# A decoder layer on one core: the GLU and the conv's gates become a stage of seven-product pairs ahead of the attention

## The chip, the cores and the metric

The kernel runs on one core of one Trainium2 chip. The metric is the time of one execution in microseconds (us), measured on the device; the median of three runs of the kernel before is 1817.19 us. The engines are named as in the profile: PE (TensorE, matmuls), PEld (its weight loads), DVE (VectorE), ACT (ScalarE), POOL (GpSimd) and SP (SyncE, which here only issues DMAs). Each engine works through its own instructions in a fixed order. ACT and POOL issue DMAs too, from the same queues as their arithmetic, so a DMA that can't be issued yet holds up what stands behind it.

## The reference

One layer of a hybrid decoder for 1024 tokens of width 1024, all in float32.

```
h = rms_norm(x)
q, k, v (12 heads of 128), glu_in (2*1024), gates (2*1024) = split(h @ w_in)
a   = dilated window attention: 3 groups of 4 heads, dilation 1, 4, 16; merged over the groups
y_a = a @ w_attn_out
c   = c_val * sigmoid(c_gate)                    # the GLU, glu_in = [c_val | c_gate]
c   = causal depthwise conv of 31 taps over c
y_c = silu(layer_norm(c)) @ conv_pw_w
mixed = sigmoid(g_a + b) * y_a + sigmoid(g_c + b) * y_c
x   = x + rms_norm(mixed @ w_out)
u   = conv of 3 taps over rms_norm(x) @ w_up     # 2 * 2816 columns
x   = x + rms_norm((gelu(u_gate) * u_val) @ w_down)
```

## The kernel before, in words

Channels lie on the 128 partitions and tokens along the free dimension, in two halves of 512. Every float32 product is made of three matmuls: each operand is split into a high part (ACT, line 166) and a low remainder (DVE, line 167), and high*high, high*low and low*high are added up in PSUM (`mm3`, lines 185 to 188). A block of 128 output channels and 512 tokens over 1024 input channels takes 24 matmuls of 128x512.

The order of the instructions on each engine is chosen at compile time by a planner, which takes the instructions in the order of the program as priorities and moves a later one forward where an engine would otherwise be free. `tc.high_priority(offset=-LAG)` puts the conv's taps 2000 places back, so that they fill what DVE has left. Inside `tc.manual_schedule()` the order is the written one.

The stages, in order:

- Norm of x (lines 211 to 235). The rows are normed and transposed into `hTh` and `hTl`. ACT issues the loads of the small tables (lines 122 to 127) in between.
- Attention (lines 244 to 451). Per group, `values_of` projects v in two halves through the two PSUM tiles `pp`, and then come four heads. `head` projects q and k (96 matmuls, through `pp`) and `core` does scores, softmax and values. The bias table goes from `sel` through DRAM (`vscr`, `bscr`), with DMAs on ACT's queue (lines 250 to 258). Between the heads stand the eight GLU blocks: `glu(m)` projects gate and value (96 matmuls), takes the sigmoid, multiplies, and hands the tile to the conv on DVE (31 taps, lines 268 to 272). `conv_out` (line 275) transposes a finished conv and stores it into `convn` in DRAM. At the end `gates(mp, 1, ..)` projects the conv's gates (384 matmuls) and stores them into `sigc`.
- Middle (lines 454 to 569). Its pool of tiles stands where the attention's stood. `weights` loads the row sums (line 470) and makes the groups' weights; `gates(mp, 0, ..)` projects the attention's gates (384 matmuls), with two `merge(n)` behind each pair of blocks. A merge loads 128 tokens of all heads (`ld`, line 492), weights and adds them on DVE, and transposes them (line 499) into `aTh` and `aTl`. Then come `y_a`, the layer norm with its transposes (`norm_half`) and the pointwise projection.
- Output projection and norms (lines 572 to 672). The last lines build sums and differences of blocks of the normed activations (T1 to T4).
- Up-projection. Two of 22 pairs of blocks go plainly (`up_plain`), the other 20 as `Seven` (line 760): a pair of 128 output channels by 1024 tokens over 1024 channels is a 2 by 2 block product, and it is made of seven block products instead of eight, each of 12 matmuls. Four sums of weight blocks are made on POOL (line 770), seven splits on ACT and DVE, and what PSUM holds is copied and added between the products (`take`). The steps have written times (`AT`, line 757): one product per step, splits five steps ahead.
- Down-projection, last norm and output.

Of the kernel before, what the change touches and what calls it, by code (L numbers as in the profile page):

```python
# [78 lines left out]
def trunk_kernel(ctx: ExitStack, tc: tile.TileContext, a, out):  # L79
# [41 lines left out]
    def small_loads():  # L121
        nc.scalar.dma_start(ffn_g, a["ffn_g"])
        nc.scalar.dma_start(conv_w, a["conv_w"])
        nc.scalar.dma_start(conv_b, a["conv_b"])
        nc.scalar.dma_start(gate_b, a["gate_b"])
        nc.scalar.dma_start(ffn_w, a["ffn_w"])
        nc.scalar.dma_start(ffn_b, a["ffn_b"])
# [71 lines left out]


    with ExitStack() as mix:
# [8 lines left out]

        with tc.tile_pool(name="xs", bufs=1) as xs:
            xt = [dt() for _ in range(NT)]
            for i in range(NT):
                nc.sync.dma_start(xt[i], a["x"][i * P:(i + 1) * P, :])
            nc.scalar.dma_start(mix_g, a["mix_g"])
            hTh += [dt(F32R) for _ in range(KC)]
            hTl += [dt(F32R) for _ in range(KC)]
            first_w = None
            for T0, n in ((0, 1), (1, 3), (4, 4)):
                rows = xt[T0:T0 + n]  # L220
                ss = xs.tile([P, 4], F32, tag="ss", name="ss", bufs=2)
                for t in range(n):
                    sq = xs.tile([P, D], F32, tag="sq", name="sq", bufs=2)
                    nc.scalar.activation(sq, rows[t], AF.Square, accum_out=ss[:, t:t + 1])
                r = rsqrt_of(ss[:, :n], 1.0 / D, RMS_EPS, xs, f"rx{n}", n)
                for t in range(n):
                    if n == 4 and t == 3:
                        nc.scalar.mul(rows[t], rows[t], r[:, t:t + 1])
                    else:
                        nc.vector.tensor_scalar(rows[t], rows[t], r[:, t:t + 1], None, op0=ALU.mult)  # L230
                ts = slice(T0 * P, (T0 + n) * P)
                transposed(rows, lambda k: (hTh[k][:, ts], hTl[k][:, ts]), mix_g)
                if not first_w:
                    first_w = [load_v(0, k) for k in range(4)]
            small_loads()

# [5 lines left out]
        bscr = dram.tile([12, P, BW[0]], F32, name="bscr")  # L242

        with tc.tile_pool(name="att", bufs=1) as att:
# [5 lines left out]
            nc.scalar.dma_start(relb[0:32, :], a["rel_bias"])  # L250
            nc.scalar.dma_start(sel, a["sel"])
# [4 lines left out]
            nc.scalar.dma_start(vscr, vrow)  # L256
            for g in range(3):
                nc.scalar.dma_start(  # L258
                    bscr[4 * g:4 * g + 4, :, :BW[g]],
                    vscr[4 * g:4 * g + 4, BOFF[g]:BOFF[g] + BW[g]].unsqueeze(1).to_broadcast((4, P, BW[g])))  # L260
# [4 lines left out]
            def conv(m, cin):  # L265
                acc = att.tile([P, S], F32, tag="acc", name="acc", bufs=2)
                with tc.high_priority(offset=-LAG):
                    nc.vector.tensor_scalar(acc, cin[:, 0:S], conv_w[:, m, 0:1], conv_b[:, m:m + 1],
                                            op0=ALU.mult, op1=ALU.add)
                    for k in range(1, TAPS):  # L270
                        nc.vector.scalar_tensor_tensor(acc, cin[:, k:k + S], conv_w[:, m, k:k + 1], acc,  # L271
                                                       op0=ALU.mult, op1=ALU.add)
                ready.append((m, cin, acc))

            def conv_out():

                m, nat, acc = ready.pop(0)
                for q in range(2):
                    pt = ps_tile((P, 4, P), "pt")
                    for k in range(4):  # L280
                        nc.tensor.transpose(pt[:, k, :], acc[:, (4 * q + k) * P:(4 * q + k + 1) * P], ident)
                    nc.scalar.copy(nat[:, q * 512:(q + 1) * 512], pt.rearrange("p a b -> p (a b)"))
                nc.gpsimd.dma_start(
                    convn.rearrange("(n p) (m c) -> p n m c", p=P, c=P)[:, :, m, :],
                    nat[:, 0:S].rearrange("p (n c) -> p n c", c=P))

            def glu(m):
                w = load_pair(a["w_glu"][m], 4)
                pv, pg = pp_tile(), pp_tile()
                cin = att.tile([P, TAPS - 1 + S], F32, tag="cin", name="cin", bufs=2)  # L290
                project(w, 1, h_in, pg)
                nc.scalar.activation(cin[:, TAPS - 1:], pg, AF.Sigmoid)
                project(w, 0, h_in, pv)
                nc.vector.memset(cin[:, 0:TAPS - 1], 0.0)
                nc.vector.tensor_mul(cin[:, TAPS - 1:], pv, cin[:, TAPS - 1:])
                conv(m, cin)
# [14 lines left out]
            def values_of(g):  # L311
# [4 lines left out]
                for half in range(2):  # L316
                    pv = [pp_tile() for _ in range(2)]
                    for k in range(KC):
                        wh, wl = first_w[k] if (g, half) == (0, 0) and k < 4 else load_v(g, k)
# [111 lines left out]
            for g in range(3):  # L431
                vt = values_of(g)
                for j in range(NH):
                    head(g, j, vt, 0 if j % 2 == 0 else len(ready) if (g, j) == (2, 3) else min(len(ready), 1))
                    for m in glus.get((g, j), ()):
                        glu(m)
# [530 lines left out]
```

## Time and profile before

| | |
|---|---|
| three runs | 1815.9, 1817.19, 1818.48 us |
| the profiled execution | 1822.72 us, of which the span of the profile 1820.6 us |
| PE busy | 1767.3 us, 97% of the span, 8152 matmuls |
| DVE busy | 1177.1 us, 65% |
| ACT busy | 720.7 us, 40% |
| POOL busy | 215.4 us, 12% |
| mean granted clock of TensorE | 0.988 |

A row of the timeline gives start, duration, engine, line, operation, tiles and count, and in brackets the time that the engine was idle before it and what ended that. A row of the windows gives the busy time of each engine in a stretch (and its instructions), then the granted clock as a share of 2.4 GHz, the busy share of the DMA engines and GB/s. A matmul's own duration overlaps the next one's: what one costs is the distance between two starts. An engine named with a q (ACTq, SPq) issues DMAs.

### The profile page before, as it was taken

Reading aid. Unit: us, or ns where it says so; the run is one execution under the profiler, and the core shown is the slowest. Engines: PE = TensorE matmul, PEld = TensorE weight load, DVE = VectorE, ACT = ScalarE, POOL = GpSimd, SP = SyncE. Lnnn points to the kernel's source line nnn. Section 1 sums busy time; section 2 is a strip of 40 time slices with the busy share of each in tenths; the row PEclk is TensorE's granted clock in tenths of the full one; section 3 lists DMA queues with packets and bytes.
Section 4 is the critical chain, followed back from the end, with each engine's and each line's share of the span. In section 5 each row is a group of like instructions: output and inputs, shape, how many; then the busy total and the mean of one; then the engine's idle time right before and its main releaser. Section 6 shows DMA issues by size and latency. Waiting matters only on the chain.

```text
span 1820.6 us, 22184 instructions
## 1 busy us (share of the span) xinstructions
PE 1767.3 (97%) x8152; PEld 1483.4 (81%) x8152; DVE 1177.1 (65%) x1967; ACT 720.7 (40%) x1331; POOL 215.4 (12%) x241
## 2 busy tenths in 40 slices
PE   7899999999989999999999999999999999999997
PEld 5688889788988888888888888778888888788886
DVE  6239979339682587947574457857667676873524
ACT  6232343243422333222442244555455555653322
POOL 0000010021100000000000000342332323120000
PEclk9999999999999999999999999999999999999998
DMA  5321133121321222235333143243323333683532
GB/s 193 111 50 51 46 85 95 35 77 48 89 76 29 68 58 82 93 109 183 116 102 118 57 146 116 83 132 99 110 87 101 98 91 128 202 286 114 179 99 93
DMA packets 84285, 188.21 MB, mean 103 GB/s; under 512 B 11331, under 2 KB 13267, under 8 KB 84176
## 3 DMA queue, kind: packets, MB, share of 16 engines
q1 hardware_dynamic: 67536, 139.75, 25.1%
q0 software_dynamic: 13392, 43.46, 7.3%
q10 hardware_dynamic: 3248, 3.58, 0.6%
q8 instruction: 64, 1.05, 0.2%
q14 instruction: 45, 0.37, 0.1%
HBM read 149.90 MB, written 38.94 MB: 104 GB/s over the span
## 4 chain that ended last, share of the span: by engine, by line
PE 61%; issue 29%; DVE 3%; POOL 3%; DMA 2%; ACT 1%; ACTq 1%; SPq 0%; POOLq 0%; DVEq 0%
PE ps L710 10%; PE pp L186 10%; PE pp L187 10%; PE pp L188 10%; PE po L710 6%; PE pt L710 4%; PE ps L188 1%; PE ps L187 1%; PE ps L186 1%; PE pp L710 1%; POOL oscr L416 1%; ACTq L258 1%; POOL mscr L416 1%; PE po L188 1%; PE pt L188 1%
## 5 line engine op out<-in xcount | busy, mean ns | idle before, releaser
L186 PE MATMUL pp<-d,wh 128*128 128x512 f32 x1088 | 430.0, 396 | 15.1 <-DVE d L332 14.8
L188 PE MATMUL pp<-d,wl 128*128 128x512 f32 x1088 | 428.9, 394 | 0.0
L187 PE MATMUL pp<-d,wh 128*128 128x512 f32 x1088 | 428.7, 394 | 0.0
L271 DVE SCALAR_TENSOR_TENSOR acc<-cin,conv_w,acc 128x1024 f32<-128x1024 f32 x240 | 305.4, 1283 | 4.6 <-issue 1.5
L186 PEld LDWEIGHTS pp<-d,wh 128*128 128x128 f32 x1088 | 206.2, 189 | 58.0 <-issue 15.7
L188 PEld LDWEIGHTS pp<-d,wl 128*128 128x128 f32 x1088 | 206.1, 189 | 41.7
L187 PEld LDWEIGHTS pp<-d,wh 128*128 128x128 f32 x1088 | 206.3, 190 | 41.2
L167 DVE TENSOR_TENSOR wl<-wr,wh 128x512 fp32r<-128x512 f32 x200 | 136.9, 689 | 153.8 <-ACT wh L166 152.7
L166 ACT CAST wh<-wr 128x512 fp32r<-128x512 f32 x200 | 123.5, 623 | 266.9 <-PE pp L187 164.0
L710 PE MATMUL ps<-d,wh 128*128 128x512 f32 x592 | 182.6, 389 | 1.3 <-ACT ps L786 1.3
L167 DVE TENSOR_TENSOR wl<-wq,wh 128x512 fp32r<-128x512 f32 x148 | 119.3, 814 | 93.5 <-ACT wh L166 93.5
L166 ACT CAST wh<-wq 128x512 fp32r<-128x512 f32 x148 | 91.5, 624 | 129.5 <-PE pt L188 100.9
L710 PEld LDWEIGHTS ps<-d,wh 128*128 128x128 f32 x592 | 111.1, 188 | 24.8 <-ACT ps L786 1.7
L167 DVE TENSOR_TENSOR wl<-ws,wh 128x512 fp32r<-128x512 f32 x80 | 63.7, 799 | 81.6 <-ACT wh L166 81.6
L710 PE MATMUL ps<-d,wl 128*128 128x512 f32 x296 | 115.3, 389 | 0.0
L687 DVE SCALAR_TENSOR_TENSOR u<-u,ffn_w 128x1023 f32<-128x1023 f32 x88 | 112.7, 1281 | 3.3 <-ACT u L681 1.9
L710 PE MATMUL po<-d,wh 128*128 128x512 f32 x336 | 103.6, 389 | 0.0
L187 PE MATMUL pp<-wl,d 128*128 128x512 f32 x232 | 91.0, 392 | 1.8 <-DVE wl L167 1.8
L188 PE MATMUL pp<-wh,d 128*128 128x512 f32 x232 | 90.7, 392 | 0.0
L186 PE MATMUL pp<-wh,d 128*128 128x512 f32 x232 | 89.6, 392 | 0.7 <-ACT u L616 0.7
L325 PE MATMUL pp<-wh,d 128*128 128x512 f32 x192 | 80.1, 418 | 3.0 <-DVE d L332 3.0
L326 PE MATMUL pp<-wl,d 128*128 128x512 f32 x192 | 79.3, 413 | 0.0
(300 smaller groups left out, 2958.4 us busy)
## 6 DMA issues: line engine op xcount, KB each, us to landing
wq<-in_w_up_dram SPq DMA_DIRECT2D x100, 256.0 KB, 2.7
wq<-in_w_down_dram SPq DMA_DIRECT2D x88, 256.0 KB, 3.2
wr<-in_w_v_dram SPq DMA_DIRECT2D x48, 256.0 KB, 2.8
wr<-in_w_qk_dram SPq DMA_DIRECT2D x48, 256.0 KB, 2.7
fscr<-u POOLq DMA_DIRECT2D x22, 512.0 KB, 2.9
d<-fscr POOLq DMA_DIRECT2D x44, 256.0 KB, 5.0
wr<-in_w_glu_dram SPq DMA_DIRECT2D x32, 256.0 KB, 2.7
wr<-in_w_gate_dram SPq DMA_DIRECT2D x32, 256.0 KB, 2.8
```

What stands on the lines that cost most here:

```text
L166: nc.scalar.copy(hi, raw)
L167: nc.vector.tensor_sub(lo, raw, f(hi))
L186: nc.tensor.matmul(ps, lh, rh, start=first, stop=False)
L187: nc.tensor.matmul(ps, lh, rl, start=False, stop=False)
L188: nc.tensor.matmul(ps, ll, rh, start=False, stop=last)
L258: nc.scalar.dma_start(bscr[4 * g:4 * g + 4, :, :BW[g]], vscr[4 * g:4 * g + 4, BOFF[g]:BOFF[g] + BW[g]].unsqueeze(1).to_broadcast((4, P, BW ...
L271: nc.vector.scalar_tensor_tensor(acc, cin[:, k:k + S], conv_w[:, m, k:k + 1], acc, op0=ALU.mult, op1=ALU.add)
L325: nc.tensor.matmul(ps, hTh[k][:, sl], wh, start=k == 0, stop=False)
L326: nc.tensor.matmul(ps, hTh[k][:, sl], wl, start=False, stop=False)
L416: nc.gpsimd.dma_start(dst[:, r, :, g, j, :], src[:, 2 * r:2 * r + 2, :])
L687: nc.vector.scalar_tensor_tensor(o[:, d:], src[:, :S - d], ffn_w[:, c, k:k + 1], o[:, d:], op0=ALU.mult, op1=ALU.add)
L710: nc.tensor.matmul(ps, wp[:, cs], xp, start=first and k == 0 and n == 0, stop=last and k == 3 and n == 2, skip_group_check=open_)
```

## The change

The eight GLU pairs and the four pairs of the conv's gates move into a stage of their own between the norm and the attention. There GLU 0 and 1 are made plainly, first for tokens 0 to 511 (whose rows are loaded and normed first), then for tokens 512 to 1023; between them the blocks of h and the sums T1 to T4 are built, into 16 tiles. Then GLU 2 to 7 and the four pairs of gates go as ten pairs of seven products, with the class `Seven` moved up and shared with the up-projection. The GLU tiles 2 to 7 are stored to DRAM (`cinscr`). The taps of convs 0 and 1 stand in this stage's written order, one tap per step. The attention keeps convs 2 to 7, loaded from `cinscr`, and no GLU. The attention's gates are projected half at the end of the attention (two pairs, before the last `conv_out`) and half in the middle, one pair ahead of merges 0 to 3 and one ahead of merges 4 to 7. The small tables and the bias table's DMAs are issued on POOL's queue.

```diff
-        nc.scalar.dma_start(ffn_g, a["ffn_g"])
+        nc.gpsimd.dma_start(ffn_g, a["ffn_g"])
...
+    def product(ps, w, X, x, first, last, open_=False):
+
+        for k in range(4):
+            cs = slice(k * P, k * P + P)
+            xh, xl = X[x, k]
+            for n, (wp, xp) in enumerate(((w[0], xh), (w[0], xl), (w[1], xh))):
+                nc.tensor.matmul(ps, wp[:, cs], xp, start=first and k == 0 and n == 0,
+                                 stop=last and k == 3 and n == 2, skip_group_check=open_)
...
+    def weave(pairs, sum_tile, extra=()):
+
+        todo = list((at, rank, -1, what) for at, rank, what in extra)
+        for n, pair in enumerate(pairs):
+            pair.n, pair.sum_tile = n, sum_tile
+            todo += [(7 * n + at, rank, n, what) for at, rank, what in pair.steps()]
+        with tc.manual_schedule():
+            for *_, what in sorted(todo, key=lambda x: x[:3]):
+                what()
...
+            for cin in cins:
+                nc.gpsimd.memset(cin[:, 0:TAPS - 1], 0.0)
+            glu_plain(0)
+            for i in range(4, 8):
+                nc.sync.dma_start(xt[i], a["x"][i * P:(i + 1) * P, :])
+            rows = norm_rows(4, 4)
...
+            wide = [u_tile() for _ in range(4)]
...
+            glu_plain(1)
...
+            class Glu(Mix):
+                def after(self):
+                    g = lambda: self.gate
+                    return ((13, lambda: nc.scalar.activation(g(), g(), AF.Sigmoid)),
+                            (14, lambda: nc.vector.tensor_mul(g(), g(), self.val)),
+                            (15, lambda: nc.gpsimd.dma_start(cinscr[self.j], g())))
...
+            for m, at in ((0, 3), (1, 40)):
+                cin = cins[m]
+                extra.append((at, 0, conv_start))
+                for i in range(TAPS):
+                    extra.append((at + i, 4.5, lambda m=m, cin=cin, i=i: list(conv_taps(m, cin, acc[0]))[i]()))
...
+            weave([Glu(a["w_glu"][m], X, m) for m in range(2, KC)] + [Gates(a["w_gc"][m], X, m) for m in range(4)],
+                  lambda: pre.tile([P, 512], F32, tag="ws", name="ws", bufs=4), extra)
...
-            nc.scalar.dma_start(vscr, vrow)
+            nc.gpsimd.dma_start(vscr, vrow)
...
-            glus = {(0, 0): [0], (0, 1): [1], (0, 3): [2], (1, 1): [3], (1, 3): [4], (2, 1): [5], (2, 3): [6, 7]}
+            convs = {(0, 0): [2], (0, 2): [3], (1, 0): [4], (1, 2): [5], (2, 0): [6], (2, 2): [7]}
...
-            for mp in range(4):
-                gates(mp, 1, lambda m, sg: nc.sync.dma_start(sigc[m], sg))
-                if mp % 2:
-                    conv_out()
+            for mp in range(2):
+                gates(mp)
+            while ready:
+                conv_out()
...
-            for mp in range(4):
-                gates(mp, 0, ga.__setitem__)
-                merge(2 * mp)
-                merge(2 * mp + 1)
+            for n in range(NT):
+                if n % 4 == 0:
+                    gates(2 + n // 4)
+                merge(n)
```

## Rows read from the trace of the kernel before

**Rows 1.** The page: busy time (share of the span) and instructions.
```profile
PE 1767.3 (97%) x8152; PEld 1483.4 (81%) x8152; DVE 1177.1 (65%) x1967; ACT 720.7 (40%) x1331; POOL 215.4 (12%) x241
```
**Rows 2.** The chain that ended last, in the up-projection: start, us, what.
```profile
1361.28 2.72 PE pt L710 x12
```
**Rows 3.** Windows: stretch, length, busy us of each engine (count), clock, DMA share, GB/s.
```profile
76.50:83.40 6.90, 3.17 (x8) 2.53 (x9) 3.87 (x6) 3.38 (x6) 0.00 (x0) 0.51 0.36 120
...
80.20:720.00 639.80, 628.42 (x3054) 544.76 (x3055) 429.38 (x653) 216.51 (x474) 47.00 (x63) 0.98 0.22 62
...
650.00:675.00 25.00, 25.00 (x130) 21.24 (x129) 23.57 (x39) 9.11 (x27) 0.84 (x1) 1.00 0.19 43
...
1131.70:1203.50 71.80, 67.07 (x308) 54.82 (x307) 55.09 (x101) 36.50 (x71) 30.61 (x20) 1.00 0.37 118
1203.50:1527.00 323.50, 323.50 (x1429) 267.88 (x1428) 228.92 (x241) 175.50 (x259) 99.59 (x88) 1.00 0.33 99
1527.00:1600.00 73.00, 71.21 (x306) 58.25 (x306) 57.81 (x70) 47.01 (x69) 16.09 (x27) 0.98 0.58 192
```
**Rows 4.** Timeline of PE: matmuls that waited, and for what.
```profile
80.23 0.77 PE L186 MATMUL pp<-d,wh 128*128 128x512 f32 x1 [8.78 <-DVE d L332]
...
541.70 0.77 PE L186 MATMUL pp<-d,wh 128*128 128x512 f32 x1 [3.03 <-DVE d L332]
...
1156.76 0.50 PE L710 MATMUL pp<-d,wh 128*128 128x512 f32 x1 [2.35 <-DVE d L640]
...
1559.96 0.50 PE L187 MATMUL pp<-wl,d 128*128 128x512 f32 x1 [1.79 <-DVE wl L167]
```
**Rows 5.** Timeline of ACT: behind the DMAs of its own queue.
```profile
8.63 1.06 ACT L224 ACTIVATE sq<-d 128x1024 f32<-128x1024 f32 x1 [1.90 <-DMA conv_w<-in_conv_w_dram]
...
51.85 11.04 ACTq L258 DMA_DIRECT2D bscr<-vscr  x3
63.02 1.14 ACT L166 CAST wh<-wr 128x512 fp32r<-128x512 f32 x2 [11.38 <-PE pp L327]
```
**Rows 6.** Groups by line and shape: busy us, mean ns | idle before, releasers.
```profile
L271 DVE SCALAR_TENSOR_TENSOR acc<-cin,conv_w,acc 128x1024 f32<-128x1024 f32 x240 | 305.4, 1283 | 4.6 <-issue 1.5
L167 DVE TENSOR_TENSOR wl<-wr,wh 128x512 fp32r<-128x512 f32 x200 | 136.9, 689 | 153.8 <-ACT wh L166 152.7 <-PE pt L281 0.7
...
L167 DVE TENSOR_TENSOR wl<-ws,wh 128x512 fp32r<-128x512 f32 x80 | 63.7, 799 | 81.6 <-ACT wh L166 81.6
...
L770 POOL TENSOR_TENSOR ws<-wq 128x512 f32<-128x512 f32 x40 | 57.7, 1464 | 10.0 <-DMA wq<-in_w_up_dram 7.3 <-DVE wl L167 2.3
```
**Rows 7.** Timeline of POOL: one weight sum while DVE never paused.
```profile
1180.08 7.69 POOL L770 TENSOR_TENSOR ws<-wq 128x512 f32<-128x512 f32 x1 [0.57 <-DVE wl L167]
```
**Rows 8.** Timelines of PE, POOL, SP and DVE from the last conv to the last merge.
```profile
788.76 3.92 DVE L271 SCALAR_TENSOR_TENSOR acc<-cin,conv_w,acc 128x1024 f32<-128x1024 f32 x3
...
809.13 0.60 PE L281 MATMUL pt<-ident,acc 128*128 128x128 f32 x4
...
817.03 0.90 POOL L283 DMA_DIRECT2D convn<-cin  x1 [35.45 <-ACT cin L282]
823.04 0.89 POOL L470 DMA_DIRECT2D mls<-mscr  x1 [5.12 <-DMA convn<-cin]
...
822.42 0.80 SPq L492 DMA_DIRECT2D ld<-oscr  x2
...
830.54 0.19 DVE L472 TENSOR_TENSOR wsum<-mls 128x32 f32<-128x32 f32 x1 [20.10 <-DMA mls<-mscr]
...
892.76 0.69 DVE L496 TENSOR_TENSOR ld<-ld 128x512 f32<-128x512 f32 x1
...
900.66 0.60 PE L499 MATMUL ps<-ident,ld 128*128 128x128 f32 x4
901.10 0.60 PE L499 MATMUL pt<-ident,ld 128*128 128x128 f32 x4
```
**Rows 9.** Windows: line 271 (the taps) alone; DVE busy (count).
```profile
80.20:720.00 639.80, 246.21 (x193) 0.98 0.22 62
```

More of the change, by code (lines that the diff above doesn't have):

```diff
@@ L208, in trunk_kernel @@
         h_in = full(hTh, hTl)
[L211 to L235, printed above, removed]
         convn = dram.tile([S, D], F32, name="convn")
@@ L263, in trunk_kernel, with conv @@
             ready = []
-            def conv(m, cin):
+            def conv(m):
+                cin = att.tile([P, TAPS - 1 + S], F32, tag="cin", name="cin", bufs=2)
                 acc = att.tile([P, S], F32, tag="acc", name="acc", bufs=2)
+                nc.gpsimd.memset(cin[:, 0:TAPS - 1], 0.0)
+                nc.gpsimd.dma_start(cin[:, TAPS - 1:], cinscr[m])
                 with tc.high_priority(offset=-LAG):
[L268 to L272, printed above, removed]
+                    for tap in conv_taps(m, cin, acc):
+                        tap()
                 ready.append((m, cin, acc))
@@ L278, in conv_out @@
                 for q in range(2):
[L279 to L296, printed above, removed]
+                    conv_half(nat, acc, q)
+                conv_store(m, nat)
             def perm(ap, g):
@@ L433, in trunk_kernel, with gates @@
                 for j in range(NH):
[L434 to L439 removed]
+                    head(g, j, vt, j % 2 if (g, j) != (2, 3) else 0)
+                    for m in convs.get((g, j), ()):
+                        conv(m)
+            ga = {}
+            def gates(mp):
+                w = load_pair(a["w_gate"][mp], 4)
                 for c in range(2):
@@ L695, in quadrant @@
         def quadrant(j, q):
-            raw = raw_tile(j < 2)
+            raw = raw_tile(True)
             nc.sync.dma_start(raw, a["w_up"][j, q])
             return raw
-        def wsplit(raw):
-            return split(raw, (P, 512), wpool, "w", 7)
-        def product(ps, w, x, first, last, open_=False):
-            for k in range(4):
-                cs = slice(k * P, k * P + P)
-                xh, xl = X[x, k][:, 0], X[x, k][:, 1]
-                for n, (wp, xp) in enumerate(((w[0], xh), (w[0], xl), (w[1], xh))):
-                    nc.tensor.matmul(ps, wp[:, cs], xp, start=first and k == 0 and n == 0,
-                                     stop=last and k == 3 and n == 2, skip_group_check=open_)
         def up_plain(js):
```

280 lines of the change are left out of this document (208 added, 72 removed).

## The prediction

> **What bounds the kernel now.** I read the page first. PE is busy for 97% of the span [rows 1]: the kernel pays for PE's instructions one after the other, and besides them only for the few places where PE waits. So I need three things: what one matmul costs, where PE waits, and which of these places the change touches.
>
> The price is in the chain of waits: in the up-projection's steady stretch every product of 12 matmuls takes 2.72 us, 227 ns a matmul [rows 2], and through 323 us of it PE is busy without a gap, though DVE does 229 us of work there [rows 3]. A seven-product stage can thus run at PE's own pace.
>
> The waits are in PE's timeline [rows 4]. The largest is 8.78 us, at 80.23, where the first head needs a PSUM tile that DVE has not yet drained. Four more of its kind stand at the other two groups' values; the last, 3.03 us at 541.70, is shown. After such a wait the clock is down: from 76.5 to 83.4 it is 0.51 of full speed, which is the level of 1.2 GHz, so that 6.9 us cost 3.4 us [rows 3].
>
> **The sum, part by part.** All terms are changes of the profiled execution's 1822.72 us (span 1820.6 and 2.1 around it). That one is 5.5 us, 0.3%, above the median of the runs, 1817.19, and I carry the difference over.
>
> 1. *Fewer matmuls.* Ten pairs of blocks take seven products instead of eight: 10 x 2.72 = 27.2 us less on PE. If the 1152 matmuls that leave the heads cost a nanosecond or two more than 227 there (an estimate, no row separates them), it is 1 to 2 more: I take -28 (bounds -27 and -30).
>
> 2. *The start.* ACT sat idle for 1.90 us ahead of the third square, with the small tables' DMAs in its queue [rows 5]. They leave it. What is late next is the fourth row tile, since the rows now come in two batches of four. -1 (0 to -1.9). On POOL's queue they hold up only memsets.
>
> 3. *Building T1 to T4.* The up-projection does the same at 1131 to 1203 us: two plain pairs on PE, beside them 16 operands on ACT and DVE. PE was busy 67.07 of 71.80 us there [rows 3], the longest wait 2.35 us for a split [rows 4]. I take the same, +4.7. Below, nothing, if the four rows normed late are early enough; above 15, three times what the row shows, because squares, norm and transposes of these rows now fall into the 22 us of the first plain half, and because the first gate tile must wait until a `wide` tile is free, which T4 ends.
>
> 4. *The weave.* Per pair of GLU and 19.04 us of PE, DVE has what it has per pair of the up-projection, 228.92 / 17 = 13.5 us [rows 3], less four taps and plus seven at 1.283 [rows 6]: 13.5 + 3 x 1.283 = 17.3 us. That fits, at 91%. POOL's sums take (57.7 - 7.7) / 39 = 1.28 us but for one [rows 6, 7], and the row of the splits shows that they cost DVE something: 689 ns while POOL rests, 799 on the sums [rows 6]. I take +4; the bounds are 0 and 23 (the rival below).
>
> 5. *The end of the weave.* Where the up-projection goes over into the down-projection PE idled 1.79 us [rows 4] and the clock was at 0.98 over 73 us [rows 3], some 1.5 us more: +3.3 (0 to 6). Here values follow, which take their weights through the same tiles.
>
> 6. *The first group's values.* ACT spent 11.04 us on issuing the three bias DMAs, and its casts stood behind them for 11.38 [rows 5]; the weights came late, then the drain, and PE paid 8.78 [rows 4] and 3.4 for the clock. With the DMAs on POOL that cause goes. What is late next is the drain itself with the taps of convs 2 and 3 in DVE's queue, as at the other groups: about 3 us and perhaps the clock. -7 (0 to -12.2).
>
> 7. *The merges.* This is the term that decides. Before, the conv's gates end at 809.1 and the last `conv_out` begins [rows 8]. Its store is issued at 817.03; the first tile of the middle, SP's `ld`, is issued at 822.42 though its data have long been in DRAM, and POOL's `mls` waits 5.12 us for that store's landing [rows 8]: the middle's pool opens only when the attention's last tile is let go. Then `mls` lands at 830.5, weights, four rounds of two loads, and DVE ends the last merge at 893.5; PE has transposed it at 901.4 [rows 8]. From `conv_out` to `y_a` it is 92.3 us. PE had 4 x 21.8 = 87 us of the attention's gates to do meanwhile, and idled nowhere. After the change two of the four pairs are spent before `conv_out`, which stands behind them in the program. They can't be saved for later, because the last head's core needs them as filling. What is left for PE is 2 x 21.8 = 43.6, the transposes of six merges (24 x 0.11 = 2.6), `y_a`'s first halves for two PSUM tiles (24 x 0.227 = 5.4) and norm_half's transposes (32 x 0.11 = 3.5): 55. The chain is shorter when PE waits for it: the 7 us between the last add (893.5) and its transposes (900.66) go, and of the 7.9 from `conv_out` to its store [rows 8] some 6, since 8 transposes and two copies need 0.9 and 1.1 us [rows 5, 8]: 79. So PE waits 79 - 55 = 24, less about 1 for each of the three rounds before the last, whose transposes stood behind matmuls too: 21. With 3.4 for the clock [rows 3] I take +24. Bounds: 45, if the chain keeps 92 and only 47 covers it, and 5, if the rounds shrink to the loads and adds alone.
>
> 8. *The heads.* DVE does 429 us in the 640 us of heads and values [rows 3], 246 of them taps [rows 9]. Six convs bring 6 x 31 x 1.283 = 239; the splits of 24 weight tiles at 0.69 and the products go: about 400. PE loses six to eight GLUs of 21.8 us there: 466 to 509 are left, so DVE comes to 79 to 86%. Taps fill gaps only, and between two heads without a GLU, at 650 to 675, PE was fully busy beside a DVE at 23.57 of 25 us [rows 3]. 0 (0 to 15, one tap for each of 12 heads).
>
> Sum: -28 - 1 + 4.7 + 4 + 3.3 - 7 + 24 = 0. I forecast no change: **1817 us**.
>
> **The rivals.**
>
> *The merge chain is covered.* The chain from `conv_out` to `y_a` could shrink to what its loads and adds need, or the planner could put `conv_out` ahead of the second pair of gates once its taps are done. For it: DVE will have ended conv 7 well before, since the cin tiles come from DRAM and not from a GLU. Against it: before, `conv_out` began only behind the last gates' matmul, at 809.1, though its taps were done at 792.7 [rows 8]. Term 7 at 6 instead of 24: 1799 us.
>
> *The taps and the sums fight in the weave (slower).* At 1180 one POOL sum took 7.69 us [rows 7] instead of 1.28, while DVE worked without a pause beside it, and splits wait for POOL in turn [rows 6]. If taps and sums can't run at once, a GLU pair needs 17.3 + 4 x 1.28 - 0.8 (7 x 0.11, the waits already in 13.5) = 21.6 us of DVE and POOL together, against 19.04 of PE. This decides from 19.04 on, for the 62 steps that hold a tap, 8.9 pairs: 8.9 x 2.6 = 23 in place of 4, 1836 us. Against it: 323 us of the up-projection show no PE wait [rows 3], but with four taps per pair. The Trainium skill speaks for this rival: "SBUF — State Buffer", section "Who interferes with whom", says that a VectorE instruction with two SBUF inputs and a GpSimd instruction that reads SBUF shut each other out for a whole instruction, whichever was first. The 7.69 agrees; whether a tap does it, no row here shows. By the rule the time would be this rival's.
>
> *DVE is the bound in the heads (slower).* At up to 86% its order, fixed at compile time, may cost the upper bound of term 8: 15 us, 1832. Against it stands the stretch from 650 [rows 3].
>
> *It doesn't do what it says.* Too few tiles or late sums, and the weave's products don't reach 2.72: at 3 us, 70 x 0.28 = 20 more, 1837.
>
> **How the numbers follow.** What can be told from no change is 0.2%, 3.6 us. The forecast, with its own range from 1807 to 1827, has 0.45: 0.12 faster, 0.21 same, 0.12 slower. The covered chain has 0.26, all faster. The fight has 0.18, the heads 0.08, both slower; the last 0.03, of which 0.02 within the bounds of the same. Together: faster 0.38, same 0.23, slower 0.39. The range reaches to the centres of the rivals at both sides and a little on: 1798 to 1842, with about a tenth left out at each end.
>
> **What would show it.** Term 1: 8032 matmuls, and products of 2.72 us in the chain of waits. Term 6: no DMA of `bscr` on ACT, and a wait of 3 us or less ahead of the first head. Term 7: PE waiting, some 20 us in all, between the end of the last attention gates and `y_a`, with `aTl` or `ld` as what it waited for; if PE has no gap there, the forecast is wrong by 20 us. The fight: POOL sums longer than 2 us, and products in the weave waiting for `wl`. I am wrong if the time leaves 1807 to 1827, and most so if it falls because nothing in the middle waits.

## The result and the profile after

The changed kernel takes 1833.57 us (median of four runs, 1831.07 to 1835.66) against 1817.84 for the kernel before: 0.9% more, a ratio of 1.0087 with a 95% interval of 1.007 to 1.0105. It is slower, by 16 us. No change had been forecast. The time lies within the wide range, 1798 to 1842, but outside the 1807 to 1827 that the forecast gave itself. It is nearest to two rivals, the heads bound by DVE (1832) and the fight of taps and sums (1836); what follows shows that neither was the cause.

The first line of the page: PE has the 120 matmuls less that were worked out, 20.1 us less of busy time, and a span that is 13.3 us longer. So it waits more than before [rows 1].

```profile
PE 1747.2 (95%) x8032; PEld 1464.1 (80%) x8032; DVE 1257.8 (69%) x2048; ACT 762.8 (42%) x1430; POOL 324.6 (18%) x325
```

In the chain of waits (start, us, what) a product of the new stage costs what one of the up-projection cost [rows 2]:

```profile
118.47 2.72 PE ps L220 x12
```

The windows of the changed kernel, with the columns of [rows 3]: the start, the building of T1 to T4, the stage of seven products, the first group's values, the merges.

```profile
0.00:57.15 57.15, 35.33 (x156) 27.87 (x156) 27.82 (x76) 32.01 (x59) 5.86 (x15) 1.00 0.37 129
57.15:98.70 41.55, 35.24 (x149) 27.98 (x150) 41.55 (x52) 19.72 (x36) 24.22 (x10) 0.96 0.22 64
98.70:278.10 179.40, 179.14 (x798) 148.01 (x797) 155.70 (x153) 76.90 (x128) 72.99 (x47) 1.00 0.33 107
308.00:345.00 37.00, 27.43 (x105) 22.17 (x106) 32.49 (x36) 7.70 (x13) 1.56 (x3) 0.83 0.46 139
879.30:930.00 50.70, 31.40 (x131) 24.34 (x130) 39.03 (x107) 19.64 (x50) 0.00 (x0) 0.76 0.36 119
```

The new stage runs well: PE is busy for 179.14 of 179.40 us. In the building DVE has no pause (41.55 of 41.55). At the values and the merges PE idles for 9.6 and 19.3 us, and the clock is down besides. The waits behind that, in PE's timeline with what ended them:

```profile
69.80 0.80 PE L220 MATMUL pp<-d,wh 128*128 128x512 f32 x1 [4.02 <-DVE d L407]
...
308.15 0.72 PE L552 MATMUL pp<-wh,d 128*128 128x512 f32 x1 [3.34 <-DVE d L559]
...
341.19 0.76 PE L186 MATMUL pp<-d,wh 128*128 128x512 f32 x1 [9.42 <-DVE d L559]
...
512.59 0.47 PE L186 MATMUL pp<-d,wh 128*128 128x512 f32 x1 [4.52 <-DVE d L559]
...
891.64 0.48 PE L727 MATMUL ps<-ident,ld 128*128 128x128 f32 x1 [6.56 <-DVE ld L724]
...
910.68 0.48 PE L758 MATMUL po<-ident,nat 128*128 128x128 f32 x1 [4.93 <-DVE d L731]
```

The wait at the first head, 8.78 us before [rows 4], is still there, with 9.42. To compare whole stages I count what each one loses: its length less its matmuls at the price of undisturbed running (227 ns for 128x512, 121 for 128x256, 61 for 128x128, 109 for a transpose; the medians of the distance from one start to the next). That holds waits and half clock together.

| stage | lost before | lost after | difference | forecast |
|---|---|---|---|---|
| 120 matmuls fewer | | | -27.2 | -28 |
| start and first plain half | 18.7 | 28.3 | +9.6 | -1 |
| building T1 to T4, second half | | 8.9 | +8.9 | +4.7 |
| seven products | | 0.6 | +0.6 | +4 |
| end of that stage, first group's values | 10.9 | 17.3 | +6.4 | +3.3 - 7 |
| heads and the other values | 44.5 | 33.2 | -11.3 | 0 |
| merges, up to the pointwise projection | 1.3 | 27.9 | +26.6 | +24 |
| the rest | 22.3 | 22.0 | -0.3 | 0 |
| sum | | | +13.3 | 0 |

### The profile page after: what moved, and what is told of

Same layout as the page of the kernel before. It is cut to its first block, busy times and chain, and to the rows that moved or that the text cites. A ratio compares the mean times of both kernels' runs of the same rounds, so it can differ in the third digit from the quotient of the medians.

```text
span 1833.9 us, 22282 instructions
## 1 busy us (share of the span) xinstructions
PE 1747.2 (95%) x8032; PEld 1464.1 (80%) x8032; DVE 1257.8 (69%) x2048; ACT 762.8 (42%) x1430; POOL 324.6 (18%) x325
## 4 chain that ended last, share of the span: by engine, by line
PE 85%; DVE 7%; DMA 4%; issue 2%; ACT 1%; POOL 0%; SPq 0%; DVEq 0%; POOLq 0%; ACTq 0%
PE ps L220 15%; PE pp L186 12%; PE pp L187 12%; PE pp L188 12%; PE po L220 9%; PE pt L220 7%; PE pp L220 2%; PE ps L188 2%; DVE acc L311 2%; PE ps L186 2%; PE ps L187 2%; PE pp L552 1%; PE pp L553 1%; PE pp L554 1%; DMA cin<-cinscr 1%
## 5 line engine op out<-in xcount | busy, mean ns | idle before, releaser
L186 PE MATMUL pp<-d,wh 128*128 128x512 f32 x704 | 278.5, 398 | 15.7 <-DVE d L559 14.9
L220 PE MATMUL ps<-d,wh 128*128 128x512 f32 x904 | 279.4, 390 | 2.9 <-ACT ps L252 2.6
L187 PE MATMUL pp<-d,wh 128*128 128x512 f32 x704 | 278.2, 395 | 1.6 <-DVE d L731 1.6
L188 PE MATMUL pp<-d,wl 128*128 128x512 f32 x704 | 278.4, 395 | 0.0
L186 PEld LDWEIGHTS pp<-d,wh 128*128 128x128 f32 x704 | 133.8, 191 | 43.3 <-issue 14.5
L187 PEld LDWEIGHTS pp<-d,wh 128*128 128x128 f32 x704 | 133.9, 190 | 28.7 <-DVE d L731 2.1
L188 PEld LDWEIGHTS pp<-d,wl 128*128 128x128 f32 x704 | 133.6, 190 | 27.0
L220 PE MATMUL pt<-d,wh 128*128 128x512 f32 x392 | 121.4, 389 | 0.5 <-ACT u L417 0.5
L220 PEld LDWEIGHTS po<-d,wh 128*128 128x128 f32 x512 | 96.0, 188 | 20.0
L220 PE MATMUL po<-d,wl 128*128 128x512 f32 x256 | 99.6, 389 | 0.0
L220 PEld LDWEIGHTS ps<-d,wl 128*128 128x128 f32 x452 | 84.9, 188 | 17.6
L187 PE MATMUL pp<-wl,d 128*128 128x512 f32 x232 | 91.0, 392 | 1.8 <-DVE wl L167 1.8
```

What stands on the lines that cost most here:

```text
L186: nc.tensor.matmul(ps, lh, rh, start=first, stop=False)
L187: nc.tensor.matmul(ps, lh, rl, start=False, stop=False)
L188: nc.tensor.matmul(ps, ll, rh, start=False, stop=last)
L220: nc.tensor.matmul(ps, wp[:, cs], xp, start=first and k == 0 and n == 0, stop=last and k == 3 and n == 2, skip_group_check=open_)
```

## The experiments

Every kernel is the changed one with the edit that is named. Ratios are to the kernel before, which ran on the same chip beside it; the changed kernel has 1.0087, and 0.001 is 1.8 us.

**1. The squares' scratch tile.** In the changed kernel the squares of the row norm write into the ring of 32 tiles, where before they had a pool of their own. In ACT's timeline the squares of rows 1 to 3 (line 353) begin at 15.66, behind five casts of weights, two of which wait for their DMAs; in the kernel before the third square ran at 8.63 [rows 5].

```profile
14.32 0.62 ACT L166 CAST wh<-wr 128x512 fp32r<-128x512 f32 x1 [1.08 <-DMA wr<-in_w_glu_dram]
...
15.66 1.05 ACT L353 ACTIVATE d<-d 128x1024 f32<-128x1024 f32 x1
```

```diff
-                    sq = dt()
+                    sq = u_tile()
```

> Only the scratch tile of the row squares is another one, so that ACT squares rows 1 to 3 ahead of the weight casts. Theory A (the start lost about 10 us because ACT's order puts the squares of rows 1 to 3 behind casts that wait for weights): the first long run of GLU matmuls begins at about 24 instead of 32.7 us, and the time is 1833.6 - 7 to 10 = 1824 to 1827. Theory B (the start is late because weights and row tiles share the DMA engines): no change, 1832 to 1835.

Measured: 1.0093 (1.0078 to 1.0108), no change. The order on ACT did change, and the second plain half begins at 53.62 instead of 57.15: 3.5 us of the 9.6. They had not reached the end: the merges' first wait ended at 891.56, as in the changed kernel (891.64). Theory A is right about the place and wrong about the size, and a gain early in the kernel is not yet a gain.

**2. The last conv before the last core.**

```diff
-                    head(g, j, vt, j % 2 if (g, j) != (2, 3) else 0)
+                    head(g, j, vt, j % 2)
```

The changed kernel's timelines of PE, POOL and SP show what the forecast had in mind: the last conv is transposed at 839 and 846, between the gates' matmuls, its store is issued at 847.63, and the first loads of the middle (line 720) at 851.80.

```profile
839.49 0.60 PE L318 MATMUL pt<-ident,acc 128*128 128x128 f32 x4
...
845.88 0.60 PE L318 MATMUL pt<-ident,acc 128*128 128x128 f32 x4
...
847.63 0.90 POOL L322 DMA_DIRECT2D convn<-cin  x1 [19.48 <-issue]
852.27 0.89 POOL L698 DMA_DIRECT2D mls<-mscr  x1 [3.74 <-PE pp L188]
...
851.80 0.81 SPq L720 DMA_DIRECT2D ld<-oscr  x2
...
879.18 0.80 SPq L720 DMA_DIRECT2D ld<-oscr  x2
...
892.78 0.33 SPq L720 DMA_DIRECT2D ld<-oscr  x1
```

The conv's taps end at 721, so nothing but the program's order holds it. And the loads come in rounds of two, the second and third at 879.18 and 892.78, since a round's tiles come free only when PE has transposed them.

> The last conv_out moves ahead of the last head's core (its taps are done at 721, the changed kernel transposes it at 839 to 846). Theory A (the middle opens when the last conv's store lands, 847.6 + 2): the middle opens at about 830, PE's waits between 879 and 930 fall from some 26 us to under 12, and the time is 1814 to 1820. Theory B (the chain is bound by the four rounds of two merge loads, 13 us each, wherever it begins): the waits stay above 20 us and the time is 1829 or more.

Measured: 1.0050 (1.0033 to 1.0068), 1825.09 us. Between the theories: the middle opens at 842.09, 10 us earlier and not 20, as the last core itself now ends later, and 12.5 us of waits remain between 886 and 911.

**3. The conv's loads on SP's queue.** Conv 3's load stands in POOL's queue behind the bias DMAs, and DVE stands still for 4.44 us on it, with splits and drains behind (DVE's timeline; the drains are line 559):

```profile
319.87 0.81 DVE L308 TENSOR_SCALAR acc<-cin,conv_w,conv_b 128x1024 f32<-128x1024 f32 x1 [4.44 <-DMA cin<-cinscr]
...
335.57 1.28 DVE L311 SCALAR_TENSOR_TENSOR acc<-cin,conv_w,acc 128x1024 f32<-128x1024 f32 x1
336.77 0.68 DVE L559 TENSOR_TENSOR d<-pp,d 128x512 fp32r<-128x512 f32 x1
337.37 1.27 DVE L311 SCALAR_TENSOR_TENSOR acc<-cin,conv_w,acc 128x1024 f32<-128x1024 f32 x1
338.56 0.68 DVE L167 TENSOR_TENSOR wl<-wr,wh 128x512 fp32r<-128x512 f32 x1
339.16 1.28 DVE L311 SCALAR_TENSOR_TENSOR acc<-cin,conv_w,acc 128x1024 f32<-128x1024 f32 x1
340.36 1.28 DVE L559 TENSOR_TENSOR d<-pp,d 128x512 fp32r<-128x512 f32 x2
```

```diff
-                nc.gpsimd.dma_start(cin[:, TAPS - 1:], cinscr[m])
+                nc.sync.dma_start(cin[:, TAPS - 1:], cinscr[m])
```

> The loads of convs 2 to 7 go on SP's queue instead of POOL's, where conv 3's stands behind the three bias DMAs. Theory A (DVE stands still for 4.44 us on that load, and the splits and drains behind it come late): the wait of 9.42 us at 341 falls to 5 or less, 1826 to 1830. Theory B (the drains stand behind taps whatever the load does): the wait stays at 8 to 10 us, 1832 to 1835. If the loads hold up weights in SP's queue, it is slower than 1835.

Measured: 1.0122 (1.0107 to 1.0137), slower. The wait at the first head falls from 9.42 to 5.16, as theory A says, but the one in the middle of the values grows from 3.34 to 4.42, and later heads wait more (2.12 us at 481, 2.30 at 691). That it was the weights behind the loads in SP's queue was expected but not shown.

**4. All attention gates in the middle.**

```diff
-            for mp in range(2):
-                gates(mp)
...
-                if n % 4 == 0:
-                    gates(2 + n // 4)
+                if n % 2 == 0:
+                    gates(n // 2)
```

> All four pairs of the attention's gates stand in the middle again, one ahead of every two merges, and none at the end of the attention. Theory A (the merges' 26 us are lack of matmuls beside them): no wait of over 3 us between the end of the last head and y_a, but the last head's core runs without filling and loses 10 to 20 us: 1818 to 1829. Theory B (the chain has become longer by itself): waits of 15 us or more remain in the merges and the core loses as well, 1838 or more.

Measured: 1.0093 (1.0074 to 1.0112), no change. Neither theory: the planner moved gates forward into the last core anyway, and PE then stands 19.50 us in one piece at 859.47 ahead of the first merge's transposes. Where the program writes the gates made no difference here: the core takes its filling either way, and what is left is too little for the chain.

**5. A shorter merge chain.** On top of experiment 2 the groups' weights are made at the attention's end, in tiles that outlive its pool, and three loads are in flight.

```diff
+    beta = const.tile([P, NT, 3, NH], F32, name="beta")
+    wsum = const.tile([P, NT, NH], F32, name="wsum")
...
+                mls = att.tile([P, 256], F32, tag="bias", name="bias", bufs=2)[:, :NT * 24].rearrange(
+                    "p (n g j e) -> p n g j e", g=3, j=NH, e=2)
...
-                ld = mid.tile([P, 3, NH, HD], F32, tag="ld", name="ld", bufs=2)
+                ld = mid.tile([P, 3, NH, HD], F32, tag="ld", name="ld", bufs=3)
```

> On top of the last conv_out before the last core: the groups' weights are made at the attention's end (their small tiles outlive the pool), and three merge loads are in flight instead of two. Theory A (what is left of the merge wait is the chain's own latency, 12 us from the opening to the first multiplication and 13 us a round of two loads): y_a begins 10 us or more earlier than at 912, waits and clock together fall from 21 to under 10 us, and the time is 1808 to 1817. Theory B (PE simply lacks matmuls there; DVE's merging, 8 times 3.3 us and the drains, sets the pace): 1822 to 1826.

Measured: 0.9965 (0.9954 to 0.9977), 1812.61 us, faster than the kernel before. Theory A. The two halves apart are experiment 15.

**6. The bias table early.** Its matmuls and DMAs go to the first plain half of the GLU.

```diff
-            sel = att.tile([33, BCOLS], F32, tag="cin", name="sel", bufs=2)
-            vrow = att.tile([12, BCOLS], F32, tag="cin", name="vrow", bufs=2)
+            sel = pre.tile([P, S], F32, tag="acc", name="acc", bufs=1)[:33, :BCOLS]
+            vrow = u_tile()[:12, :BCOLS]
```

> The bias table is written to DRAM during the first plain half of the GLU, so that neither its DMAs nor its two tiles stand in the way of convs 2 and 3 at the first values. Theory A (the 9.42 us at 341 come from conv 3's load, late behind the bias DMAs, on which DVE stands still): the wait falls to 4 or less, with it the half clock of 10 us, and the time is 1822 to 1828. Theory B (the drains of the values stand behind taps of two convs in DVE's queue in any case): the wait stays above 7 us, 1831 to 1835.

Measured: 1.0099 (1.0081 to 1.0118), no gain. Both convs' loads are there at 302 now, and PE waits at the values all the same, in two places:

```profile
315.79 0.76 PE L552 MATMUL pp<-wh,d 128*128 128x512 f32 x1 [7.27 <-DVE d L559]
...
345.73 0.76 PE L186 MATMUL pp<-d,wh 128*128 128x512 f32 x1 [5.12 <-DVE d L559]
```

Theory B: the drains alternate with taps, as in the rows of experiment 3, whenever both convs are there.

**7. The bias DMAs back on ACT.** This undoes one part of the change.

```diff
-            nc.gpsimd.dma_start(vscr, vrow)
+            nc.scalar.dma_start(vscr, vrow)
```

and so for the table's other DMAs.

> The bias table's five DMAs go back to ACT's queue, as before the change; all else is the changed kernel. If the move to POOL's queue had saved what the prediction said (7 us), this is 1838 to 1842, with a wait of 12 us or more at the first head. If the move only put the stall into another queue, it is 1831 to 1836, with ACT's casts late instead of conv 3's load.

Measured: 1.0166 (1.0151 to 1.0181): 14 us slower than the changed kernel, more than either theory. The same three DMAs that take POOL 3.28 us to issue take ACT 12.83, and ACT's drain and casts wait behind them; PE's wait among the values is 13.18 us instead of 3.34 (timelines of the changed kernel's POOL, then of this kernel's ACT and PE):

```profile
304.56 3.28 POOL L501 DMA_DIRECT2D bscr<-vscr  x3 [3.69 <-DMA vscr<-vrow]
```

```profile
300.04 12.83 ACTq L501 DMA_DIRECT2D bscr<-vscr  x3
312.91 0.58 ACT L558 CAST d<-pp 128x512 fp32r<-128x512 f32 x1 [13.54 <-issue]
...
317.36 0.77 PE L552 MATMUL pp<-wh,d 128*128 128x512 f32 x1 [13.18 <-DVE d L559]
```

So the move to POOL's queue was right. It did not help against the wait that was there before, because another one took its place.

**8. The start.** The squares as in experiment 1, and all eight row tiles loaded ahead of the weights, as before the change.

```diff
-            for i in range(4):
+            for i in range(NT):
                 nc.sync.dma_start(xt[i], a["x"][i * P:(i + 1) * P, :])
```

> The squares have another scratch tile and all eight row tiles are loaded ahead of the weights. Theory A (the start and the building of T1 to T4 wait for rows that are normed late): the GLU's matmuls begin at 23 or earlier, the wait of 4 us at 70 shrinks to under 2, and the time is 1824 to 1829. Theory B (the building is bound by DVE, which works without a pause from 57 to 110, and PE's order puts the late rows' transposes behind the plain half): that wait stays and the time is 1830 to 1835.

Measured: 1.0064 (1.0048 to 1.0081). The second plain half begins at 48.41, 8.7 us earlier than in the changed kernel: that is most of the 9.6 us of the start. The wait of 4 us in the building stays and the time is in theory B's range, but the start came out as in theory A. Of the 8.7 us the time shows 4, and the intervals overlap.

**9. Taps held back from the values.**

```diff
-                nc.gpsimd.memset(cin[:, 0:TAPS - 1], 0.0)
+                nc.scalar.copy(cin[:, 0:TAPS - 1], pad)
...
+                if (g, j) == (0, 0):
+                    nc.scalar.mul(pad, f(qh)[:, 0:TAPS - 1], 0.0)
```

> The pads of convs 2 to 7 are copied from a tile that the first head writes, so that no tap can stand in DVE's queue among the first group's values. Theory A (the drains of the values stand behind taps): the waits of 3.34 us at 308 and 9.42 at 341 fall below 2 us together and the half clock there goes; 12 to 17 us less, minus up to 6 if the taps crowd the heads later: 1817 to 1826. Theory B (the drains are slow by themselves, ACT's casts and DVE's subtractions in turn): the waits stay above 8 us in sum, 1830 or more.

Measured: 1.0103 (1.0079 to 1.0126), no gain, though the mechanism is theory A's: the two waits are down from 12.8 us to 4.3 and PE reaches the first head 11.7 us earlier (PE's timeline):

```profile
305.36 0.47 PE L553 MATMUL pp<-wh,d 128*128 128x512 f32 x1 [2.12 <-DVE d L560]
...
329.53 0.47 PE L186 MATMUL pp<-d,wh 128*128 128x512 f32 x1 [2.13 <-DVE d L560]
```

Most of it is given back at 452 to 475, where the fourth head's core meets a conv that is due and has almost no matmuls of the next group's values between its steps: PE is busy for 16.88 of 23 us, at a clock of 0.70 (window of this kernel):

```profile
452.00:475.00 23.00, 16.88 (x83) 14.48 (x82) 16.26 (x36) 12.54 (x37) 3.84 (x5) 0.70 0.27 76
```

**13. The same, with each conv transposed one head later.**

```diff
-                    head(g, j, vt, j % 2 if (g, j) != (2, 3) else 0)
+                    head(g, j, vt, int(j % 2 == 0 and (g, j) != (0, 0)))
```

> As the run with held taps, but each finished conv is transposed one head later. Theory A (the held taps cost nothing by themselves; the wait went to the head where the conv was due too soon, at 453 to 470): the small waits there and their half clock of 13.65 us go, and the time is the changed kernel's minus 10 to 17, 1817 to 1824. Theory B (DVE is full in the heads, and 35 us of taps taken out of the values can't be placed anywhere): waits move to other heads and the time is 1830 or more.

Measured: 1.0031 (1.0018 to 1.0044), 10 us below the changed kernel. Theory A. The windows at the values and at the core (this kernel, the columns as above):

```profile
308.00:345.00 37.00, 34.87 (x147) 28.37 (x146) 8.76 (x13) 8.24 (x14) 1.86 (x4) 0.95 0.45 140
452.00:475.00 23.00, 21.53 (x104) 20.83 (x103) 15.36 (x24) 10.81 (x25) 2.11 (x3) 1.00 0.53 161
```

At the values DVE does 8.76 us instead of 32.49 and PE idles 2.1 instead of 9.6. In the core PE has the next group's values between its steps (104 matmuls instead of 83), as in the changed kernel, and the clock stays up. The later transposes were not run without the held taps. But PE reaches the first head at 332.99 instead of 341.19 and at full clock, before any transpose that was moved, so the gain is that of the held taps:

```profile
332.99 0.47 PE L186 MATMUL pp<-d,wh 128*128 128x512 f32 x1 [2.13 <-DVE d L560]
```

**12. The new stage without its taps.**

```diff
-                for i in range(TAPS):
+                for i in range(1):
                     extra.append((at + i, 4.5, lambda m=m, cin=cin, i=i: list(conv_taps(m, cin, acc[0]))[i]()))
```

> The changed kernel without the taps 1 to 30 of convs 0 and 1 in the stage of seven products (these two convs are left out of the result). Theory A (PE sets the pace of that stage, DVE and POOL have room, whatever they cost each other): within 2 us of the changed kernel, 1831 to 1836, with products of 2.72 us as before. Theory B (the predicted fight of taps and sums costs its 23 us there): 1815 or less, with POOL's sums back at 1.3 us.

Measured: 1.0084 (1.006 to 1.0108): the same. POOL's sums take 1.3 us again, as all but one did in the up-projection [rows 6, 7] (groups by line and shape from 110 to 283, one of a pair's four sums, first of the changed kernel, then of this one):

```profile
L237 POOL TENSOR_TENSOR ws<-wr 128x512 f32<-128x512 f32 x7 | 13.3, 1893 | 0.0
```

```profile
L237 POOL TENSOR_TENSOR ws<-wr 128x512 f32<-128x512 f32 x7 | 9.4, 1346 | 0.0
```

and DVE does half of its work there (83.64 us instead of 155.70), while PE is as busy as before:

```profile
98.70:278.10 179.40, 179.40 (x801) 148.49 (x800) 83.64 (x94) 77.30 (x128) 49.09 (x45) 1.00 0.33 108
```

So taps and sums do slow each other down, and it costs nothing. The Trainium skill's rule ("SBUF — State Buffer", section "Who interferes with whom"), of which the prediction left open whether it holds for taps, agrees with these rows: a tap has two inputs in SBUF, and this sum takes 1893 ns beside taps and 1346 without them. What the rule says nothing of is the slack that the stage has.

Why the fight's sum came out too large can be seen in DVE's rows of the changed kernel, from 110 to 283. The additions of PSUM (lines 259 and 261) keep their length, while a split of the new stage takes up to 1130 ns on the mean, against the 689 of splits while POOL rests [rows 6]:

```profile
L167 DVE TENSOR_TENSOR wl<-wq,wh 128x512 fp32r<-128x512 f32 x16 | 18.1, 1130 | 1.1 <-ACT wh L166 1.1
...
L259 DVE TENSOR_TENSOR u<-po,u 128x512 f32<-128x512 f32 x5 | 3.4, 683 | 0.0
```

The rival counted all of DVE's work against POOL's, also these additions, which have only one input in SBUF. Without them, 62 taps, 70 splits, six products and 40 sums at their undisturbed lengths are 62 x 1.28 + 70 x 0.69 + 6 x 1.21 + 40 x 1.28 = 186 us, an estimate, and ten pairs of PE take 190. That this is the reason is argued; no run separates the additions.

**16. T3's differences on DVE.**

```diff
-                nc.gpsimd.tensor_sub(b12[k], b22[k], b12[k])
+                nc.vector.tensor_sub(b12[k], b22[k], b12[k])
```

> The four differences for T3 are made on DVE instead of POOL. Theory A (DVE works without a pause from 57 to 99 and its operations stretch from 0.68 to 1.77 us where POOL works on SBUF beside them): four more operations of 0.68 for fewer stretched ones, PE's wait of 4.02 us at 70 shrinks to under 3 and the time is 1830 to 1833. Theory B (it is the number of DVE's operations alone): the wait grows by up to 2.7 us, 1834 to 1837.

Measured: 1.0073 (1.0052 to 1.0093), not told apart from the changed kernel. The wait of 4.02 us is gone, but one of 6.88 stands at 91.44, at the beginning of the seven products (PE and POOL):

```profile
91.44 0.79 PE L220 MATMUL ps<-d,wh 128*128 128x512 f32 x1 [6.88 <-ACT ps L252]
...
59.83 14.05 POOL L237 TENSOR_TENSOR ws<-wr 128x512 f32<-128x512 f32 x1 [54.67 <-DMA wr<-in_w_glu_dram]
```

A single sum takes 14.05 us while DVE works almost without a pause beside it. It ends at 73.88, in DVE's first pause since it began (DVE):

```profile
74.57 1.12 DVE L167 TENSOR_TENSOR wl<-ws,wh 128x512 fp32r<-128x512 f32 x1 [1.83 <-ACT wh L166]
```

The wait at 70 and the time, 1830.98, came out as theory A has them, but the time is not told apart from the changed kernel's and the waits of the whole stage are as long (7.2 us in the changed kernel, 7.6 here). So neither theory is shown; that the waits come from DVE's amount of work is read from its 41.55 of 41.55 us, and stays open as a cause.

**15, 10, 11, 14 and 17. Which half, and the sums.** Experiment 15 is 5 with two loads in flight; 10 is 5 and 8 together; 11 is 5, 8 and 9; 14 is 5, 8 and 13, with the last conv before the last core; 17 is 14 with the changed kernel's start. Their edits are those shown, but for 14 and 17, which have

```diff
-                    head(g, j, vt, j % 2 if (g, j) != (2, 3) else 0)
+                    head(g, j, vt, int(j % 2 == 0 and (g, j) != (0, 0) or (g, j) == (2, 3)))
```

> The last conv_out before the last core and the groups' weights at the attention's end, but two merge loads in flight as in the changed kernel. If the weights' latency (12 us from the opening of the middle to the first multiplication) was what remained after the earlier conv_out: 1813 to 1816, as with three loads. If the rounds of two loads set the pace: 1820 to 1825.

> The start with early squares and rows (4 us less by itself) and the middle of three merge loads and early weights (some 20 less by itself) together. If the two add up: 1807 to 1810, faster than the kernel before by 0.5 to 0.7%. If what the start wins is given back at the values, as it mostly was: 1811 to 1814.

> All three together: early rows, held taps, the shortened merge chain. If the three add up: 1833.6 - 4 - 20 - 10 = 1796 to 1802. If the held taps make DVE late in the heads: 1806 or more.

> The sum of all three edits (1803) with the convs transposed one head later, the last one before the last core. Theory A: the waits at 445 to 459 and 494 go (7 us and 3.4 of clock): 1794 to 1800. Theory B (DVE full in the heads): 1801 to 1806.

> The fastest kernel so far (1793.75) with the changed kernel's start: squares in the ring of 32 tiles, rows in two batches. Theory A (with the values and the merges mended, nothing downstream gives the start's 9 us back): 1801 to 1805. Theory B (half of it is given back as in the run with the new start alone): 1796 to 1799.

| | ratio | 95% interval | us |
|---|---|---|---|
| changed kernel | 1.0087 | 1.007 to 1.0105 | 1833.57 |
| 2: last conv early | 1.0050 | 1.0033 to 1.0068 | 1825.09 |
| 15: and weights early | 1.0014 | 1.0002 to 1.0026 | 1820.15 |
| 5: and three loads | 0.9965 | 0.9954 to 0.9977 | 1812.61 |
| 10: and the start | 0.9972 | 0.9959 to 0.9985 | 1813.38 |
| 11: and held taps | 0.9915 | 0.989 to 0.994 | 1803.14 |
| 14: and convs one head later | 0.9864 | 0.9842 to 0.9887 | 1793.75 |
| 17: 14 with the changed start | 0.9917 | 0.9891 to 0.9943 | 1803.94 |

Windows from 850 to 925 show the merge chain coming down step by step. The changed kernel, then 2, 15 and 5; PE's busy time is the second number:

```profile
850.00:925.00 75.00, 56.13 (x242) 45.09 (x241) 55.59 (x167) 24.51 (x54) 0.89 (x1) 0.84 0.45 152
```

```profile
850.00:925.00 75.00, 62.01 (x272) 49.66 (x271) 60.02 (x172) 28.72 (x62) 0.00 (x0) 0.89 0.36 128
```

```profile
850.00:925.00 75.00, 64.53 (x305) 52.48 (x303) 60.48 (x163) 29.64 (x65) 0.00 (x0) 0.93 0.40 144
```

```profile
850.00:925.00 75.00, 70.74 (x334) 58.95 (x333) 65.17 (x190) 28.97 (x65) 0.00 (x0) 0.95 0.43 150
```

All three edits of the chain have their part: 7, 6.5 and 9 us of the ratio. The start shows what experiment 8 left open. Added to 5 alone, it brings nothing (10 against 5); added last, it brings 10 us (14 against 17). It is not at the first values that it is lost: in 10 the first head begins at 334.06, in 5 at 341.57, 7.5 us later. It is gone behind the third group's values, where PE waits 4.30 us in 10 and 1.00 in 5 (PE, 10 and then 5; in 8 the wait there is 4.00):

```profile
681.20 0.47 PE L188 MATMUL pp<-d,wh 128*128 128x512 f32 x1 [4.30 <-DVE d L559]
```

```profile
683.38 0.50 PE L188 MATMUL pp<-d,wh 128*128 128x512 f32 x1 [1.00 <-DVE d L561]
```

In 14 and 17, with held taps and later transposes, no wait at the values is over 2.2 us, and the gain lasts to the end. Run 15 came out as its second theory has it, with the rounds setting the pace, though the weights' latency took 6.5 us too.

Experiment 14 is the fastest kernel: 1793.75 us, 1.4% less than the kernel before. Its page begins

```profile
PE 1737.9 (97%) x8032; PEld 1456.3 (81%) x8032; DVE 1256.0 (70%) x2048; ACT 764.4 (43%) x1437; POOL 323.7 (18%) x319
```

PE has the share of the kernel before [rows 1] with 120 matmuls less, which is what the change could have been.

## Why the prediction was wrong

*Fewer matmuls* was right, -27.2 for -28: 8032 matmuls, products of 2.72 us. *The weave* was right in its forecast and better than it: PE hides whatever DVE and POOL do to each other there (12). The two rivals nearest to the time have the wrong mechanism: the fight costs nothing (12), and the heads, which one rival had bound by DVE, won.

*The merges* were right in mechanism and size: +24 forecast, 26.6 measured, with `ld` and `aTl` as what PE waited for, and 2, 15 and 5 take 22 us of it back. The rival of the covered chain is out.

Of the steps that made the kernel slower, the one furthest off is the second, *the start*: "What is late next is the fourth row tile". It was read as a list of DMAs that leave a queue. But the change also gave the squares' scratch to the ring of 32 tiles and put weights ahead of the late rows, and ACT's order followed: the squares ran behind casts that wait for weights. The term was -1 and is +9.6; the run with both undone has 8.7 of it back at 48.41, and 17 against 14 shows 10 us at the end of the kernel.

The sixth, *the first group's values*, failed as well: "What is late next is the drain itself with the taps of convs 2 and 3 in DVE's queue, as at the other groups: about 3 us". That named the right thing and mis-sized it: the 3 us are one wait [rows 4], and each of the other groups had two, with half clock behind them. In the kernel before, at the second and the third group (PE, then a window at the first of these waits):

```profile
323.11 0.76 PE L186 MATMUL pp<-d,wh 128*128 128x512 f32 x1 [2.95 <-DVE d L332]
...
513.58 0.79 PE L325 MATMUL pp<-wh,d 128*128 128x512 f32 x1 [3.02 <-DVE d L332]
```

```profile
322.20:329.10 6.90, 6.00 (x14) 4.77 (x15) 2.05 (x4) 0.59 (x1) 0.00 (x0) 0.51 0.15 38
```

By the table's count these two groups lost 24.7 us together, 12.35 each. With that price the fifth and sixth terms would have been 3.3 + 12.35 - 10.9 = +4.7 together; forecast were -3.7, and +6.4 came. In the changed kernel a drain or split stands behind one tap of 1.28 us after the other, and the first head's wait also holds some 4 us of conv 3's late load (3: 5.16 instead of 9.42). The cause that the step removed was real (7: 14 us), but it had covered the next one. What shows the price of the taps is 13, 10 us.

*Building T1 to T4* lost 8.9 for 4.7. The row it was taken from [rows 3, 1131 to 1203] had a DVE that was busy for 55.09 of 71.80 us; here it is never idle. Taking one kind of work from POOL to DVE (16) moved the wait and settled nothing.

*The heads* were put at 0 and won 11.3 us. The values of groups two and three lose 12.2 us now (7.4 and 4.8) where they lost 24.7; the rest of that row loses 21.0, where it lost 19.8. DVE is as full there as forecast, 138.14 of 160 us, and PE hardly waits:

```profile
345.00:505.00 160.00, 159.62 (x811) 143.33 (x811) 138.14 (x203) 58.33 (x133) 10.78 (x16) 1.00 0.26 74
```

That the GLU's products and splits are gone from DVE's queue at the values is the likely reason for the gain, and no run tested it. It is luck that the forecast is not further off: without this gain the span would have grown by 24.6 us.

Together, the 13.3 us by which the span grew where 0 was forecast are 10.6 too little for the start, 10.1 for the values with the end of the weave, 4.2 for the building, 2.6 for the merges and 0.8 for the matmuls, less 11.3 too much for the heads, 3.4 for the weave and 0.3 for the rest.

## What to carry to other kernels

When a change takes one cause of a wait away, price the next one by all that it costs where it can be seen, every wait and the clock behind it, and not by one row: the drains behind taps were put at 3 us, where the other groups had lost 12 each and the first group now loses 17. When it moves a tile to another pool or a load to another place in a queue, follow the order of every engine that uses it: another scratch tile and rows loaded behind weights cost the start 9 us, where the DMAs that left ACT's queue had been put at 1. And cover is a budget: 120 matmuls saved and 384 moved ahead left a chain bare that could have been shortened at once, by 22 us, with three small edits.

## What the hardware showed that was not expected

The same three broadcast DMAs of the bias table block ACT for 12.83 us and POOL for 3.28 (11.04 on ACT in the kernel before [rows 5]). A sum on POOL that takes 1.3 us where DVE leaves it room (1346 ns on the mean in 12) took 14.05 beside a DVE at work on two SBUF inputs without a pause (16). And waits of a few us cost the clock again: over the 37 us of the window that holds the waits of 3.34 and 9.42 the granted clock is 0.83, so that it was at the lower level, 1.2 GHz, for about a third of the time (an estimate: 2 x 0.17 x 37 = 12.6 us), and over the 50.70 us of the merges it is 0.76.
